# Finer waits between scalings and additions, and two other places in VectorE's order, in an attention trunk

## The chip, the cores and the metric

The kernel runs on one core of one Trainium2 chip. The metric is the device time of one execution in microseconds (us); the median of several runs counts. TensorE does the matrix products (PE in the profile, its loads of stationary operands PEld), VectorE (DVE) and ScalarE (ACT) the elementwise work, SyncE (SP) issues most loads and stores, GpSimd (POOL) some others.

## The reference

```python
D_MODEL, SEQ, DEPTH, N_MIXERS, N_HEADS = 4096, 256, 1, 2, 32     # HEAD_DIM = 128

def attn_branch(xn, w_in, w_out):
    q, k, v, g = split(xn @ w_in, 4)                # w_in: 4096 x 16384
    o = stick_breaking_attention(q, k, v)           # per head; log-space, suffix sums over the keys
    return (o * silu(g)) @ w_out                    # w_out: 4096 x 4096

def reference(x, norm_attn, w_in_attn, w_out_attn, ..., final_norm):
    h = x
    for i in range(DEPTH):                          # DEPTH is 1: only i = 0, the attention layer
        if i % N_MIXERS == 0:
            h = h + attn_branch(rms_norm(h, norm_attn), w_in_attn, w_out_attn)
        ...
    return rms_norm(h, final_norm)
```

All is float32, for 256 rows (two tiles of 128). The convolution layer's inputs are not used at this depth.

## The kernel before, in words

**Products.** A float32 product is made of three fp32r matmuls (`mm3`): each operand is split into a high part (a cast on ScalarE: `wh<-raw`) and a low part (a subtraction on VectorE: `wl<-raw,wh`), and high x high, high x low and low x high are added in PSUM. Each weight tile that is loaded (`raw`) thus costs a cast and a subtraction before TensorE can use it.

**Units and steps.** The work is cut into 20 units, each a strip of output columns with four blocks: two tiles of rows by two blocks of 512 columns. Units 0 to 15 are the input projection (two heads' q, k, v and gate each), units 16 to 19 the output projection (1024 of the 4096 output columns each). A unit runs over the inner dimension in 16 steps. Units 0 and 16 are plain, with eight products a step. The others are "mixed": a step is either of eight products or of seven, a Strassen-like scheme in which sums of weight blocks (additions on VectorE, `raw<-raw,raw`, and accumulating loads on POOL) save one product. Such a unit gathers its products in seven PSUM banks, b1 to b7, and the four output blocks are combinations of the banks.

**Combining.** At a unit's end `combine` makes the four blocks. `two[0]` starts as a copy of bank 1 and gets bank 6 added; `two[1]` is `two[0]` plus bank 7; `one[0]` is a scaled copy of bank 1, `one[1]` a scaled copy of `two[1]`. In the attention units the scale is the row's RMS factor; there `two[1]` and `two[0]` are then scaled in place on ScalarE (`scaled`). Last, banks 2 and 4 are added to `one[0]` and `one[1]`, bank 5 to `two[1]` and `two[0]`, bank 3 to `two[0]` (`add_scaled`, a scale-and-add on VectorE in the attention units, a plain addition in the others). `nc.give("b4")` and the like free a bank for the next unit. A mixed unit's first step and its last are of eight products, into banks 2, 2, 4, 4, 5, 5, 3, 3. In the attention units `one` is `qk_sb` and `two` is `gv_sb` in the profile; in the output units both are `h`.

**Who sets the order.** The whole program is written by a planner (`Plan`). Each piece of work is a Python generator that waits for names (`nc.until`), takes and gives places in rings of buffers (`nc.take`, `nc.give`), tells names (`nc.tell`) and asks for an engine with a cost and a key. A planned engine that comes free takes, of the requests that are ready, the one with the smallest key (a planned time); an idle engine takes any. The instructions are emitted in that order, and on the chip each engine runs its own in that order, waiting only for the semaphores of its operands and buffers. A wait in the plan is therefore not a wait on the chip, but it decides which instruction stands ahead of which.

**The output units.** `blocks_out` runs in units 17 to 19, for the two columns' blocks that the unit before has made. For each column block it loads the gain of the last norm once (`grow`), and for each of the two row tiles in turn: loads the residual rows (`xres`), adds them (`h<-h,xres`), sums the squares on ScalarE (`sq<-h`), and multiplies by the gain (`h<-h,grow`, `gain_on`). The addition's key is the place of a step of the unit, `H_LATER` steps behind steps 0, 2, 4 and 6; the multiplication's is `GAIN_LATER` us behind that. `grow` and `xres` live in the ring "gh" with four places. When all is done `blocks_out` tells `("h", c)`; in the last unit `last_h` waits for that, then loads the last two gains and forms the last columns, and `finish` scales the rows by the RMS factor and stores them.

Of the kernel before, what the change touches and what calls it, by code (L numbers as in the profile page):

```python
# [61 lines left out]
SPREAD = (10, 1.0)  # L62
HEADS_AHEAD = 0
SUMS_LATER = 2
H_LATER = 6
GAIN_LATER = 8.0
ON_SCALAR = ((1, 3, 5), (1, 3))
AHEAD, SUMS_AHEAD = 6.0, 3.0
BLOCKS_LATER = 2
# [179 lines left out]
def kernel(  # L249
# [10 lines left out]
    nc = Plan(tc)  # L260
# [22 lines left out]
    OUT0 = len(units)  # L283
# [38 lines left out]
    def place_at(u, s):  # L322

        return place_of[u + int(s // NS), step_at(u + int(s // NS), int(s % NS))]
# [5 lines left out]
    def dve(emit, n, key=None, more=0, **kw):  # L330
        n = n if isinstance(n, tuple) else (n,)
        cost = sum(vector_ns(m) for m in n) + 122 * (len(n) - 1) + more
        return nc.work("vector", cost, emit, soon() if key is None else key, **kw)

    def act(emit, n, key=None, **kw):
        n = n if isinstance(n, tuple) else (n,)
        cost = sum(scalar_ns(m) for m in n) + 100 * (len(n) - 1)
        return nc.work("scalar", cost, emit, soon() if key is None else key, **kw)
# [21 lines left out]
    def together(*works):  # L360
        for w in works:
            nc.start(w)
# [346 lines left out]
    def combine(u, one, two, what):  # L709

        bank = ev[u]
        key = place_of[u + 1, 0] - SOONER * 1e3

        row = [rs["v"][:, t : t + 1] if u < OUT0 else 1.0 for t in range(NT)]

        def add(to, b, f, n):
            return dve(lambda: nc.vector.tensor_tensor(out=to, in0=bank[b], in1=f, op=ALU.add), W, key + n)

        def add_scaled(to, b, f, n, t):
            if u >= OUT0:  # L720
                return add(to, b, f, n)
            return dve(
                lambda: nc.vector.scalar_tensor_tensor(
                    out=to, in0=bank[b], scalar=row[t], in1=f, op0=ALU.mult, op1=ALU.add
                ),
                W, key + n, more=60,
            )

        def scaled(to, f, t):
            return act(lambda: nc.scalar.activation(to, f, AF.Copy, scale=row[t]), W, key - 2e3)  # L730

        yield act(lambda: nc.scalar.copy(two[:, 0, :], bank[1]), W, key - 2e3)
        yield scaled(one[:, 0, :], bank[1], 0)
        nc.give("b1")

        def early():
            yield nc.until(("full", u, 6))
            yield add(two[:, 0, :], 6, two[:, 0, :], 0)
            nc.give("b6")
            yield nc.until(("full", u, 7))  # L740
            yield add(two[:, 1, :], 7, two[:, 0, :], 0)
            nc.give("b7")
            yield scaled(one[:, 1, :], two[:, 1, :], 1)
            if u < OUT0:
                for t in (1, 0):
                    yield scaled(two[:, t, :], two[:, t, :], t)
            nc.tell(("early", u))

        def first_():
            yield nc.until(("full", u, 2))  # L750
            yield add_scaled(one[:, 0, :], 2, one[:, 0, :], 1, 0)
            nc.give("b2")
            yield nc.until(("full", u, 4), ("early", u))
            yield add_scaled(one[:, 1, :], 4, one[:, 1, :], 2, 1)
            nc.give("b4")
            nc.tell((what[0], u))

        def second():
            yield nc.until(("full", u, 5), ("early", u))
            for t in (1, 0):  # L760
                yield add_scaled(two[:, t, :], 5, two[:, t, :], 3, t)
            nc.give("b5")
            yield nc.until(("full", u, 3))
            yield add_scaled(two[:, 0, :], 3, two[:, 0, :], 4, 0)
            nc.give("b3")
            nc.tell((what[1], u))

        together(early(), first_(), second())

    def out_of(u):  # L770
# [257 lines left out]
    def load_gain(c):  # L1028
        grow[c] = wp.tile([P, W], F32, tag="gh", name=f"grow{c}", bufs=ROWS)
        return moved(  # L1030
            "sync", lambda: nc.sync.dma_start(grow[c], gain_out[:, c * W : (c + 1) * W].partition_broadcast(P)), [W],
            soon(), after=lambda: nc.tell(("grow", c)),
        )
# [13 lines left out]
    def gain_on(c, t, key=None):  # L1047
        h = hs[c, t]
        yield nc.until(("grow", c))
        yield dve(lambda: nc.vector.tensor_tensor(out=h, in0=h, in1=grow[c], op=ALU.mult), W, key)  # L1050

    def block_out(c, t, key):

        h = hs[c, t]
        yield nc.take("gh")
        yield load_out(c, t)
        yield nc.until(("xres", c, t))
        yield nc.take("att")
        yield dve(lambda: nc.vector.tensor_tensor(out=h, in0=h, in1=xres[c, t], op=ALU.add), W, key)
        nc.give("gh")  # L1060
        yield from squares(c, t, c, ALL, key)
        nc.give("att")
        yield from gain_on(c, t, key + GAIN_LATER * 1e3)

    def blocks_out(u, c):

        for d in range(2):
            for t in range(NT):
                yield nc.until(("used", u, step_at(u, 2 * (NT * d + t))), ("C", u - 1))
                if t == 0:  # L1070
                    yield nc.take("gh")
                    yield load_gain(c + d)
                key = place_at(u, 2 * (NT * d + t) + H_LATER)
                yield from block_out(c + d, t, key)
# [260 lines left out]
```

## Time and profile before

| | us |
|---|---|
| time, median of 3 runs | 1699.11 (1698.87 to 1699.47) |
| the profiled execution's own time | 1699.48 |
| its span, first to last instruction | 1697.7 |
| TensorE (PE) busy | 1681.1, 99% |
| weight loads (PEld) busy | 1417.1, 83% |
| VectorE (DVE) busy | 1602.2, 94% |
| ScalarE (ACT) busy | 1206.3, 71% |

The mean granted TensorE clock was 0.998. A row of a group gives busy time, mean time of one, and the idle time of the engine ahead of it with what ended it. A row of waits reads: who waited, for whom, us in total, times, longest. A row of the windows gives, after the window and its length, each engine's busy time with its count of instructions, the granted clock, and DMA's share and rate. A row of the timeline gives start, duration, engine, operation and, in brackets, the idle time before it and what ended it. Matmuls overlap, and their ends are modelled: the starts tell more than the busy times.

### The profile page before, as it was taken

The page shows a single profiled execution, that of the slowest core. Times are in us where ns is not written, and L with a number is a line of the kernel's source. Part 1 is how long each engine was busy: PE and PEld are TensorE (multiplying, and loading weights), DVE is VectorE, ACT ScalarE, POOL GpSimd, SP SyncE. Part 2 cuts the span into 40 slices and gives each one's busy share as a digit, 9 for nine tenths or more (in the row PEclk, how much of TensorE's full clock was granted, in tenths as well). Part 3 has the DMA queues.
Part 4 walks back from the last instruction along what each step waited for, and adds up shares of the span by engine and source line. Part 5 has one row for each costly group of instructions (what it writes and reads, how often), then busy time and mean ns, then how long its engine had stood idle before and what let it go on. Part 6 is the DMA issues. An engine that isn't in the chain of part 4 may idle for free. (4 is left out here: it accounts for less than half of the span.)

```text
span 1697.7 us, 25128 instructions
## 1 busy us (share of the span) xinstructions
PE 1681.1 (99%) x7776; PEld 1417.1 (83%) x7776; DVE 1602.2 (94%) x2025; ACT 1206.3 (71%) x1665; POOL 324.9 (19%) x400
## 2 busy tenths in 40 slices
PE   9999999999999999999999999999999999999997
PEld 7888888888888888888888888888888888888885
DVE  8889999999999999999999999999999978999997
ACT  8986767777767676767676767676867765656654
POOL 0022222122212222221222121212121111212110
PEclk9999999999999999999999999999999999999999
DMA  9979788878787879797979797979797978788895
GB/s 340 332 198 248 228 245 228 249 218 252 217 251 218 263 200 267 201 272 198 272 203 267 196 271 201 267 200 266 214 253 201 307 231 265 245 246 258 245 299 191
DMA packets 248438, 412.77 MB, mean 243 GB/s; under 512 B 28016, under 2 KB 72560, under 8 KB 248304
## 3 DMA queue, kind: packets, MB, share of 16 engines
q1 hardware_dynamic: 194544, 354.24, 62.5%
q0 software_dynamic: 53472, 56.65, 20.3%
q8 instruction: 61, 1.00, 0.2%
q14 instruction: 73, 0.60, 0.1%
q10 hardware_dynamic: 288, 0.28, 0.1%
HBM read 402.93 MB, written 8.13 MB: 242 GB/s over the span
## 5 line engine op out<-in xcount | busy, mean ns | idle before, releaser
L132 ACT CAST wh<-raw 128x1024 fp32r<-128x1024 f32 (+1 forms) x989 | 919.3, 970 | 383.8 <-DVE raw L132 166.3
L132 DVE TENSOR_TENSOR wl<-raw,wh 128x1024 fp32r<-128x1024 f32 (+1 forms) x815 | 974.3, 1217 | 50.7 <-ACT wh L132 22.7
L132 PE MATMUL acc<-wh,sh 128*128 128x512 f32 x2048 | 771.8, 389 | 1.3 <-ACT wh L132 1.3
L132 PE MATMUL acc<-wh,sl 128*128 128x512 f32 x1898 | 726.8, 383 | 0.0
L132 PE MATMUL acc<-wl,sh 128*128 128x512 f32 x1748 | 669.0, 383 | 0.0
L132 PEld LDWEIGHTS acc<-wh,sh 128*128 128x128 f32 x2048 | 383.9, 188 | 79.5 <-PE acc L132 4.7
L132 POOL DMA_DIRECT2D raw<-in_w_in_dram x300 | 258.4, 953 | 974.4 <-DMA raw<-in_w_in_dram 390.6
L132 PEld LDWEIGHTS acc<-wh,sl 128*128 128x128 f32 x1898 | 355.9, 188 | 64.4 <-DVE sl L132 0.2
L132 PEld LDWEIGHTS acc<-wl,sh 128*128 128x128 f32 x1748 | 328.4, 188 | 56.0 <-DVE wl L132 0.4
L132 DVE TENSOR_TENSOR raw<-raw,raw 128x512 f32<-128x512 f32 x348 | 236.9, 684 | 13.1 <-DMA raw<-in_w_in_dram 10.7
L132 PE MATMUL acc<-wh,oh 128*128 128x512 f32 x512 | 192.2, 383 | 0.3 <-DVE gv_sb L132 0.3
L132 PE MATMUL acc<-wh,ol 128*128 128x512 f32 x488 | 186.4, 382 | 0.0
L132 PE MATMUL acc<-wl,oh 128*128 128x512 f32 x464 | 177.4, 382 | 1.2 <-DVE wl L132 1.2
L132 DVE TENSOR_TENSOR wh<-raw,wh 128x512 fp32r<-128x512 f32 x174 | 118.9, 683 | 3.3 <-ACT wh L132 2.6
L132 DVE TENSOR_TENSOR raw<-raw 128x512 f32<-128x512 f32 x174 | 118.7, 682 | 0.0
L132 PEld LDWEIGHTS acc<-wh,oh 128*128 128x128 f32 x512 | 96.0, 187 | 17.8 <-DVE gv_sb L132 0.7
L132 PEld LDWEIGHTS acc<-wh,ol 128*128 128x128 f32 x488 | 91.4, 187 | 16.0
L132 PEld LDWEIGHTS acc<-wl,oh 128*128 128x128 f32 x464 | 87.0, 187 | 17.5 <-DVE wl L132 2.1
L132 POOL DMA_DIRECT2D raw<-in_w_out_dram x48 | 41.5, 977 | 174.0 <-DMA raw<-in_w_out_dram 62.2
L132 ACT ACTIVATE f<-f 128x384 f32<-128x384 f32 x96 | 50.5, 526 | 3.0
L132 POOL DMA_DIRECT2D p<-spill x27 | 16.5, 655 | 88.4 <-DVE ol L132 21.0
L132 DVE SCALAR_TENSOR_TENSOR gv_sb<-acc,scalars,gv_sb 128x512 f32<-128x512 f32 x45 | 33.4, 742 | 0.0
(86 smaller groups left out, 764.3 us busy)
## 6 DMA issues: line engine op xcount, KB each, us to landing
raw<-in_w_in_dram SPq DMA_DIRECT2D x1024, 256.0 KB, 4.5
raw<-in_w_out_dram SPq DMA_DIRECT2D x256, 256.0 KB, 4.5
raw<-in_w_in_dram POOLq DMA_DIRECT2D x300, 128.0 KB, 5.2
p<-spill POOLq DMA_DIRECT2D x27, 256.0 KB, 5.1
raw<-in_w_out_dram POOLq DMA_DIRECT2D x48, 128.0 KB, 5.3
xr<-in_x_dram SPq DMA_DIRECT2D x16, 256.0 KB, 5.4
xres<-in_x_dram SPq DMA_DIRECT2D x16, 256.0 KB, 5.7
out_dram<-h SPq DMA_DIRECT2D x16, 256.0 KB, 2.9
```

What stands on the lines that cost most here:

```text
L132: return self.tc.keep_in_program_order(getattr(self.engine, name)(*args, **kw))
```

## The change

Three edits. In `combine`, `early` tells its first name as soon as `one[1]` has been scaled, and a name for each of `two[1]` and `two[0]` once that one has been scaled; the addition of bank 4 waits for the first of these, and each addition of bank 5 for the name of the block that it adds to. In the output units, where nothing is scaled, these names are told at the same moment as before. `H_LATER` goes from 6 to 3 steps, `GAIN_LATER` from 8 to 30 us; both act in units 17 to 19.

```diff
-H_LATER = 6
-GAIN_LATER = 8.0
+H_LATER = 3
+GAIN_LATER = 30.0
...
             yield scaled(one[:, 1, :], two[:, 1, :], 1)
-            if u < OUT0:
-                for t in (1, 0):
+            nc.tell(("early", u))
+            for t in (1, 0):
+                if u < OUT0:
                     yield scaled(two[:, t, :], two[:, t, :], t)
-            nc.tell(("early", u))
+                nc.tell(("early", u, t))
...
         def second():
-            yield nc.until(("full", u, 5), ("early", u))
+            yield nc.until(("full", u, 5))
             for t in (1, 0):
+                yield nc.until(("early", u, t))
                 yield add_scaled(two[:, t, :], 5, two[:, t, :], 3, t)
             nc.give("b5")
```

## The prediction

> **What bounds the kernel.** I read the page's busy table first, then the waits of PE (matmuls) and of PEld (its weight loads), then the busy time in 40 us windows.
>
> ```profile
> span 1697.7 us, 25128 instructions
> ...
> PE 1681.1 (99%) x7776; PEld 1417.1 (83%) x7776; DVE 1602.2 (94%) x2025; ACT 1206.3 (71%) x1665; POOL 324.9 (19%) x400
> ...
> L132 PE MATMUL acc<-wh,sl 128*128 128x512 f32 x1898 | 726.8, 383 | 0.0
> ```
>
> ```profile
> PE acc L132 <- ACT wh L132: 1.3, 1, 1.3
> PE acc L132 <- DVE wl L132: 1.2, 2, 1.0
> PE acc L132 <- DVE gv_sb L132: 0.3, 1, 0.3
> ...
> PEld acc L132 <- PE acc L132: 4.7, 14, 0.4
> PEld acc L132 <- DVE qk_sb L132: 4.7, 14, 0.3
> ```
>
> ```profile
> 1320.00:1360.00 40.00, 39.72 (x184) 33.41 (x184) 39.97 (x49) 30.78 (x39) 6.75 (x10) 1.00 0.97 308
> ...
> 1480.00:1520.00 40.00, 39.72 (x180) 33.46 (x180) 38.86 (x45) 25.74 (x32) 7.77 (x9) 1.00 0.87 251
> ...
> 1560.00:1600.00 40.00, 39.04 (x177) 32.81 (x176) 39.24 (x48) 26.37 (x34) 7.99 (x10) 1.00 0.85 252
> ```
>
> TensorE is the bound: after the first 40 us it stands visibly in only these three windows, 0.28, 0.28 and 0.96 us, at the full granted clock (1.00). The order of work can thus win only what TensorE loses by waiting, and the tail. But a matmul counts as busy for 383 ns while the next one starts 220 ns after it, so a late start under about 160 ns shows no idle time at all. The PEld waits give these away: two kinds, 14 times each, 0.3 us a time. Fourteen is the number of borders between the attention units 1 to 15. The timeline of PE at one border (unit 9 to 10) shows what they cost:
>
> ```profile
> 850.78 0.38 PE L132 MATMUL acc<-wl,sh 128*128 128x512 f32 x1
> 851.00 0.39 PE L132 MATMUL acc<-wh,sl 128*128 128x512 f32 x1
> 851.31 0.48 PE L132 MATMUL acc<-wh,sh 128*128 128x512 f32 x1
> 851.64 0.38 PE L132 MATMUL acc<-wl,sh 128*128 128x512 f32 x1
> ...
> 852.98 0.38 PE L132 MATMUL acc<-wh,sl 128*128 128x512 f32 x1
> 853.32 0.46 PE L132 MATMUL acc<-wh,sh 128*128 128x512 f32 x1
> 853.62 0.38 PE L132 MATMUL acc<-wl,sh 128*128 128x512 f32 x1
> 853.84 0.39 PE L132 MATMUL acc<-wh,sl 128*128 128x512 f32 x1
> ```
>
> The normal step is 0.22 us (850.78 to 851.00). At 851.31 two steps in a row are 0.31 and 0.33: 0.20 us lost. At 853.32 they are 0.34 and 0.30: another 0.20 us. A unit begins with products into banks 2, 2, 4, 4, 5, 5, 3, 3, three matmuls each; the matmul at 851.00 is the sixth, so the unit began at 851.00 - 5 x 0.22 = 849.9, the first stall is the first product into bank 4, the second the first into bank 5. Both wait for the old unit's sums in these banks to be read out. Bank 5 is my reading: the view names PE there, which had long been done.
>
> **The new waits in `combine`.** The same border on VectorE, then on ScalarE:
>
> ```profile
> 846.20 0.68 DVE L132 TENSOR_TENSOR gv_sb<-acc,gv_sb 128x512 f32<-128x512 f32 x1
> ...
> 849.37 1.23 DVE L132 TENSOR_TENSOR wl<-raw,wh 128x1024 fp32r<-128x1024 f32 x1
> 850.51 0.75 DVE L132 SCALAR_TENSOR_TENSOR qk_sb<-acc,scalars,qk_sb 128x512 f32<-128x512 f32 x1
> 851.17 0.74 DVE L132 SCALAR_TENSOR_TENSOR gv_sb<-acc,scalars,gv_sb 128x512 f32<-128x512 f32 x1
> ...
> 852.43 0.74 DVE L132 SCALAR_TENSOR_TENSOR gv_sb<-acc,scalars,gv_sb 128x512 f32<-128x512 f32 x1
> ...
> 854.22 0.74 DVE L132 SCALAR_TENSOR_TENSOR gv_sb<-acc,scalars,gv_sb 128x512 f32<-128x512 f32 x1
> ```
>
> ```profile
> 846.92 0.72 ACT L132 ACTIVATE qk_sb<-gv_sb,scalars 128x512 f32<-128x512 f32 x1 [1.54 <-DVE gv_sb L132]
> 847.67 0.72 ACT L132 ACTIVATE gv_sb<-gv_sb,scalars 128x512 f32<-128x512 f32 x1
> ...
> 849.24 0.72 ACT L132 ACTIVATE gv_sb<-gv_sb,scalars 128x512 f32<-128x512 f32 x1
> ```
>
> Bank 4's addition (850.51) reads only the scaling that ended at 847.64 (846.92 + 0.72). It was placed after the last scaling (849.24 + 0.72 = 849.96), and a `wl` of 1.2 us had been taken at 849.37. PE resumed at 851.31, right behind it. The planner can now release it at about 847.8 (scaling seen; bank 4 was full at about 847.4: four products, 12 x 0.22 = 2.6 us, lie between it and 849.9). With VectorE free every 0.6 to 1.2 us, it starts by 849 and ends by 849.7, some 1.5 us before PE asks at about 851.2. Stall gone: 14 x 0.20 = 2.8 us. Bank 5 needs two additions: the first can follow from 848.8, the second only after the scaling that ends at 849.96. With one foreign instruction slipped in (at most 1.2 us) the second ends between 850.8 and 852; PE asks at about 852.9. Stall gone: another 2.8 us. Bank 3's addition (854.22) then moves forward too, to end by 854. The same at the border from unit 15 to 16: the window 1320 to 1360 has 0.28 us idle; adding the hidden 0.16 and a late second step (0.33 instead of 0.22, as at 851.64) makes 0.55; I take 0.5.
>
> No instruction is added or removed (VectorE stays at 2025, ScalarE at 1665). Displaced are the `wl` at 849.37 and its neighbours, by at most four additions, 4 x 0.66 = 2.6 us; a `wl` feeds products some microseconds ahead, and PE waited for one only twice in the whole run (1.2 us), in the out-projection. I cost this at nothing; without that cover it would be up to 2.6 us a border. The attention heads of the old unit also start some 2 us sooner: the same instructions, elsewhere.
>
> **H_LATER 6 to 3, GAIN_LATER 8 to 30.** These touch units 17 to 19. The residual addition `h<-h,xres` becomes urgent three steps (about 15 us) sooner, the multiplication by the final gain `h<-h,grow` 30 - 8 - 15 = 7 us later. A key only ranks what is ready: a free VectorE takes the multiplication anyway.
>
> ```profile
> 1578.15 0.68 DVE L132 TENSOR_TENSOR h<-h,grow 128x512 f32<-128x512 f32 x1
> ...
> 1670.26 0.69 DVE L132 TENSOR_TENSOR h<-h,grow 128x512 f32<-128x512 f32 x1
> ...
> 1673.07 1.23 DVE L132 TENSOR_TENSOR wl<-raw,wh 128x1024 fp32r<-128x1024 f32 x1 [0.99 <-ACT wh L132]
> 1674.21 1.41 DVE L132 TENSOR_TENSOR h<-acc,h 128x512 f32<-128x512 f32 x2
> 1676.31 2.50 DVE L132 TENSOR_TENSOR h<-h,xres 128x512 f32<-128x512 f32 x4 [0.69 <-ACT h L132]
> ```
>
> ```profile
> 1579.43 2.28 DVE wl L132 x2
> 1581.72 0.04 issue
> 1581.76 90.20 PE acc L132 x407
> ```
>
> The chain of waits runs through VectorE until 1581.72, then through PE: that is the 0.96 us idle, with the hidden part 1.2 us. A gain multiplication at 1578.15 stands right ahead of the `wl` that released PE; putting it later takes 0.6 us off, putting it and one neighbour later takes all. The stall in the window 1480 to 1520 (0.28, with the hidden part 0.55) may go or stay likewise. Bounds: a gain of 1.75 us and, since the sooner additions can stand before a tight `wl`, a loss of about the same. I take a gain of 0.9, nearer to the gain, because no late unit can have more than its eight such instructions ahead of the tight place and at least one is put off.
>
> In the last unit the block at 1674.21 (the last columns' sums) is planned only after the last gain (1670.26). That gain may come 1.7 us later at no cost: VectorE waits 0.99 and 0.69 us there. Each microsecond beyond moves the end. I take nothing. SP's queue is affected: a load of `xres` or of the gain waits for its buffer, and weight loads stand behind it.
>
> ```profile
> SPq L132 <- DVE h L132: 9.4, 7, 3.1
> ```
>
> Seven such waits, 3.1 us at most; seven raw buffers cover them, else it is up to 3.1 us each. POOL's reloads of `p` share these buffers and are likewise covered unless a gain is held very long.
>
> **Sum.** 2.8 + 2.8 + 0.5 + 0.9 = 7.0 us. The profiled execution took 1699.48 us (span 1697.7), 0.37 above the median of 1699.11; so 1692.5 there and 1692.1 by the median.
>
> **A rule against it.** VectorE is busy 94%, PEld 83% (first fence). The Trainium skill, "Perfetto Trace Analysis", Identifying the Most-Contended Engine, judges VectorE by its busy share but TensorE by its weight loads; by that rule VectorE is the bound, and an edit that only reorders its work brings nothing: 1699.1 instead of 1692.1. The trace speaks against it: VectorE is idle for 95 us while PE's matmuls step at 0.22 us nearly throughout; only the window 1560 to 1600 agrees.
>
> **The rivals.**
> 1. VectorE binds, so PE's stalls only move: what is won at a border is lost at the next late `wl`. For it: 39.97 of 40 us busy in 1320 to 1360. Against: its idle time elsewhere. 1699.1.
> 2. Only bank 4's stall goes; the second addition from bank 5 stays late, since its scaling still ends at 849.96 and foreign work slips in. Sum without 2.8: 1694.9.
> 3. The last unit's gain waits until its key is due, 7 us later; 1.7 are covered, 5.3 reach the output stores: 1699.1 - 7.0 + 5.3 = 1697.4.
> 4. Slower: the heads' first scores come sooner, and TensorE waits in order for ScalarE's copy of `qkT`, which stands behind a cast that waits for VectorE's sums.
>
> ```profile
> 852.60 1.05 ACT L132 CAST wh<-raw 128x1024 fp32r<-128x1024 f32 x1 [1.70 <-DVE raw L132]
> 853.55 0.58 ACT L132 COPY qkT<-tr 128x512 f32<-128x512 f32 x1
> ...
> 854.73 0.82 PE L132 MATMUL z<-qkT 128*128 128x128 f32 x4
> ```
>
> The margin is 854.73 - 854.13 = 0.6 us. If the copy keeps its place behind such a cast while the tiles to be turned are ready 2 us sooner, PE stands up to 1.7 - 0.6 = 1.1 us at each of 15 units: 16.5 us, giving 1708.6. It decides the sign from (7.0 + 3.4) / 15 = 0.7 us a unit. Against it: PE waits for no `qkT` today, and copy and scores are moved together.
>
> **Chances and range.** Forecast 0.68, rival 1 0.10, rival 2 0.10, rival 3 0.06, rival 4 0.06. About 3.4 us (0.2%) is what a measurement can tell from no change. Forecast and rival 2 are faster: 0.78; rivals 1 and 3 within it: 0.16; rival 4 slower: 0.06. The lowest time is all stalls gone: 5.6 + 0.55 + 1.75 = 7.9, so 1691.2; with 0.3 for the tail 1690.9. The top takes in rivals 2 and 3: 1697.5. The forecast's own range is 1690.9 to 1694.
>
> **What would show it.** The waits of PEld lose both rows of 14 (or one: rival 2); the steps 0.31/0.33 and 0.34/0.30 at each border become 0.22; the scale-and-add into `qk_sb` stands before the last scaling of `gv_sb`; windows 1480 to 1520 and 1560 to 1600 show PE nearer 40. The prediction is wrong if waits of PE on `z`, `tr` or `wl` appear in units 2 to 15, or if the time from the last matmul to the end grows.

## The result and the profile after

The changed kernel takes 1693.98 us (median of 8 runs, 1693.27 to 1695.18), the kernel before 1698.97 us beside it (8 runs, 1698.18 to 1699.63): a ratio of 0.9969, 95% interval 0.9960 to 0.9979, or 5.0 us. The prediction was 1692.1 us, so the gain is 2 us smaller than forecast; the median lies at the upper end of the forecast's own range, 1690.9 to 1694. The profiled execution of after took 1693.27 us, the lowest of its eight.

Span, busy table and chain on the page of after:

```profile
span 1691.6 us, 25185 instructions
...
PE 1674.7 (99%) x7776; PEld 1418.6 (84%) x7776; DVE 1600.5 (95%) x2025; ACT 1202.2 (71%) x1665; POOL 325.3 (19%) x400
...
PE 96%; DVE 2%; DMA 1%; issue 1%; ACT 0%; SPq 0%; DVEq 0%; ACTq 0%
```

The counts of the engines are those of before. 96% of the chain that ended last is now TensorE. What PEld waits for (who, for whom, us in total, times, longest):

```profile
PEld L132 <- DVE idle L132: 3.6, 10, 1.3
PEld acc L132 <- DVE sl L132: 2.3, 2, 2.1
PEld acc L132 <- DVE wl L132: 1.7, 3, 1.2
PEld acc L132 <- ACT wh L132: 0.8, 1, 0.8
```

Both rows of 14 are gone, the one on `qk_sb` and the one put down to PE. The border from unit 9 to 10 shows why. In after, unit 10 begins at 846.77. VectorE there, then ScalarE, then PE:

```profile
844.60 0.74 DVE L132 SCALAR_TENSOR_TENSOR qk_sb<-acc,scalars,qk_sb 128x512 f32<-128x512 f32 x1
845.35 0.75 DVE L132 SCALAR_TENSOR_TENSOR gv_sb<-acc,scalars,gv_sb 128x512 f32<-128x512 f32 x1
846.02 1.21 DVE L132 TENSOR_TENSOR wl<-raw,wh 128x1024 fp32r<-128x1024 f32 x1
847.15 0.74 DVE L132 SCALAR_TENSOR_TENSOR gv_sb<-acc,scalars,gv_sb 128x512 f32<-128x512 f32 x1
```

```profile
843.47 0.72 ACT L132 ACTIVATE qk_sb<-gv_sb,scalars 128x512 f32<-128x512 f32 x1 [0.98 <-DVE gv_sb L132]
...
845.79 0.72 ACT L132 ACTIVATE gv_sb<-gv_sb,scalars 128x512 f32<-128x512 f32 x1
```

```profile
849.90 0.39 PE L132 MATMUL acc<-wl,sh 128*128 128x512 f32 x1
850.13 0.38 PE L132 MATMUL acc<-wh,sl 128*128 128x512 f32 x1
850.35 0.40 PE L132 MATMUL acc<-wh,sh 128*128 128x512 f32 x1
850.58 0.39 PE L132 MATMUL acc<-wl,sh 128*128 128x512 f32 x1
```

Bank 4's addition (844.60) runs before the last scaling (845.79) and 2.2 us before the unit begins; before the change it started 0.6 us after the begin. The first product into bank 5 starts at 850.35 with the normal step. The second addition from bank 5 ended at 847.89, 2.5 us ahead of it.

Where the time went, section by section. The times are my count from the starts of the matmuls in each trace; the tail runs from the start of the last matmul to the end of the span.

| us | to unit 1 | units 1 to 16 | unit 17 | unit 18 | unit 19 | tail | span |
|---|---|---|---|---|---|---|---|
| before | 94.22 | 1350.80 | 79.21 | 80.01 | 80.56 | 12.91 | 1697.7 |
| after | 93.66 | 1345.36 | 78.63 | 79.93 | 80.46 | 13.52 | 1691.6 |
| new waits, old keys | 93.76 | 1345.06 | 78.63 | 79.75 | 81.00 | 12.73 | 1690.9 |
| new keys, old waits | 93.34 | 1351.01 | 78.63 | 80.67 | 80.72 | 16.47 | 1700.8 |
| bank 4's wait alone | 93.37 | 1344.31 | 79.19 | 80.30 | 80.59 | 12.62 | 1690.4 |
| bank 5's wait alone | 93.53 | 1359.66 | 79.19 | 80.39 | 80.67 | 12.61 | 1706.1 |
| after, root first | 93.05 | 1345.44 | 78.63 | 79.83 | 80.46 | 12.63 | 1690.0 |

The attention units give 5.44 us. Units 17 to 19 and the tail together give 252.69 - 252.54 = 0.15 us: unit 17 wins 0.58, the tail loses 0.61. The period of a unit, from its begin to the next one's, falls from 84.02 to 84.08 us (units 2 to 15) to 83.71 us (units 3 to 14).

### The profile page after: what moved, and what is told of

The parts are those of the page before. It is cut to its first block, busy times and chain, and to the rows that moved or that the text cites. A ratio compares the mean times of both kernels' runs of the same rounds, so it can differ in the third digit from the quotient of the medians.

```text
span 1691.6 us, 25185 instructions
## 1 busy us (share of the span) xinstructions
PE 1674.7 (99%) x7776; PEld 1418.6 (84%) x7776; DVE 1600.5 (95%) x2025; ACT 1202.2 (71%) x1665; POOL 325.3 (19%) x400
## 4 chain that ended last, share of the span: by engine, by line
PE 96%; DVE 2%; DMA 1%; issue 1%; ACT 0%; SPq 0%; DVEq 0%; ACTq 0%
PE acc L132 91%; PE z L132 3%; PE o L132 1%; PE tr L132 1%; DVE wl L132 1%; DVE h L132 1%; DVE raw L132 0%; DMA raw<-in_w_in_dram 0%; DMA xres<-in_x_dram 0%; ACT wh L132 0%; DMA raw<-in_w_out_dram 0%; SPq L132 0%; DVE scalars L132 0%; ACT sq L132 0%; DVE wh L132 0%
```

## The experiments

Theory A: the gain is the new waits in `combine`; the two keys give next to nothing. Rivals: the keys carry part of it; only one of the two banks matters; the gain comes from the heads' transposition of q and k ("the turn", `tr` in the profile), which moves from 2.2 us after a unit's begin to 0.36 us before it.

**New waits, old keys.** After with

```diff
-H_LATER = 3
-GAIN_LATER = 30.0
+H_LATER = 6
+GAIN_LATER = 8.0
```

> The new waits in combine alone; H_LATER 6 and GAIN_LATER 8 as before. Theory A (the two bank waits carry the gain): both rows of 14 PEld waits are gone, units 1 to 16 are 5.4 us shorter as in the changed kernel, the time is 1693.3 to 1694.0, the same as the changed kernel within 0.5 us; the stall near 1516 stays and the tail from the last matmul to the end is back at 12.9 us. Rival B (the two keys carry a part of it): 1695 to 1697.

1693.24 us (1692.53 to 1698.22), ratio 0.9973 (0.9963 to 0.9984). The whole gain is there without the keys. Unit 17 takes 78.63 us here too: the stall in the window 1480 to 1520, which the prediction had given to the keys and which I had expected to stay here, is gone. The new keys with the old waits remove it as well (78.63), and with only one of the two waits or one of the two keys it stays (79.19 to 79.35), so it can't be put down to either edit.

**New keys, old waits.** Before with `H_LATER = 3`, `GAIN_LATER = 30.0`.

> H_LATER 3 and GAIN_LATER 30 alone, the old waits in combine. Theory A: both rows of 14 PEld waits stay; unit 17 is 0.6 us shorter, unit 18 at most 0.1, and the tail 0.6 us longer if the keys cause it, so 1698.5 to 1699.2, no difference. Rival B: 1696 to 1697.5.

1702.29 us (1701.45 to 1704.87), ratio 1.0020 (1.0011 to 1.0029): slower by 3 us, which neither of my two expectations had. Both rows of 14 stay (4.8 and 4.7 us). The table puts the loss in unit 18 (+0.66) and the tail (+3.56). Its chain of waits, then POOL's timeline, then VectorE's near the end:

```profile
1564.49 6.15 DMA xres<-in_x_dram
1581.30 103.48 PE acc L132 x467
```

```profile
1624.57 0.57 POOL L132 DMA_DIRECT2D p<-spill  x1 [3.51 <-DMA xres<-in_x_dram]
```

```profile
1680.83 1.62 DVE L132 TENSOR_TENSOR h<-acc,h 128x512 f32<-128x512 f32 x3 [0.91 <-PE acc L132]
...
1684.81 0.76 DVE L132 TENSOR_TENSOR h<-acc,h 128x256 f32<-128x256 f32 x2 [1.57 <-PE acc L132]
...
1686.38 1.68 DVE L132 TENSOR_SCALAR h<-h,scalars 128x512 f32<-128x512 f32 x4
```

A load of the residual is on the chain in unit 18: the addition that was to come sooner waits for it. In unit 19 the last reload of `p` waits 3.51 us for a residual's transfer; the two share the ring of four buffers. At the end VectorE waits twice for TensorE with additions of the last columns, 0.91 us at 1680.83 and 1.57 us at 1684.81. The factor of the first rows, whose root ScalarE had ready at 1683.59, stands behind the second pair, so these rows are scaled at 1686.38, 3.6 us later than before (1682.76), where the factor stood ahead of that pair.

**Each key alone.** Before with `H_LATER = 3`, and before with `GAIN_LATER = 30.0`.

> The kernel before with H_LATER 3 alone (old waits, GAIN_LATER 8). Together the two keys cost 3.3 us, nearly all of it between the start of the last unit's final matmuls and the end. Theory G: the loss comes from the later gain, because the buffer of the gain is handed on only after its second multiplication, so the next residual load starts late. Then this run is like the kernel before, 1699 us (1698 to 1700), with the time from the last matmul's start to the end near 12.9 us. Theory H: the residual additions that come sooner push the reloads of p and the sums of the last unit back. Then this run is near 1702.3 us with some 16 us behind the last matmul.

> The kernel before with GAIN_LATER 30 alone (old waits, H_LATER 6). Theory G (late gain holds its buffer): near 1702.3 us, the time behind the last matmul near 16 us instead of 12.9. Theory H (sooner residual additions): 1699 us. If both this run and the one with H_LATER 3 are near 1699 us, the loss needs both keys, and it is an accident of the order that they make together.

1698.82 us (ratio 0.9998, 0.9989 to 1.0007) and 1697.52 us (0.9990, 0.9981 to 0.9999), tails 12.63 and 12.61 us. Neither theory G nor theory H holds: each key alone costs nothing, and the loss needs both. That is the third outcome of the expectation. The chain and the rows above show by which order the two lose; why the planner falls into it only with both was not followed further.

**Bank 4's wait alone.** Against after, with the old keys: bank 5 waits, as before the change, until both blocks have been scaled.

```diff
             yield nc.until(("full", u, 5))
+            yield nc.until(("early", u, 0))
             for t in (1, 0):
-                yield nc.until(("early", u, t))
```

> Keys as before; only the addition of bank 4 waits for its own scaling, the additions of bank 5 wait for both scalings. Theory A with the second stall at bank 5: the waits on qk_sb are gone, the other row of 14 stays, half of the gain, 1696.0 to 1696.6. Rival C (the second stall belongs to the heads' turning of tiles, which starts as soon as bank 4 is added, and not to bank 5): both rows go, 1693.3 to 1694.0.

1693.05 us (1692.30 to 1696.11), ratio 0.9966 (0.9954 to 0.9978). I had expected half the gain; it is all there. What PEld waits for, then VectorE at the same border (unit 10 begins at 845.98), then PE:

```profile
PEld L132 <- DVE idle L132: 3.6, 10, 1.3
PEld acc L132 <- DVE wl L132: 3.0, 4, 1.6
PEld acc L132 <- DVE sl L132: 1.9, 2, 1.7
```

```profile
843.79 0.75 DVE L132 SCALAR_TENSOR_TENSOR qk_sb<-acc,scalars,qk_sb 128x512 f32<-128x512 f32 x1
...
846.25 0.75 DVE L132 SCALAR_TENSOR_TENSOR gv_sb<-acc,scalars,gv_sb 128x512 f32<-128x512 f32 x1
...
847.51 0.75 DVE L132 SCALAR_TENSOR_TENSOR gv_sb<-acc,scalars,gv_sb 128x512 f32<-128x512 f32 x1
```

```profile
849.31 0.38 PE L132 MATMUL acc<-wh,sl 128*128 128x512 f32 x1
849.52 0.38 PE L132 MATMUL acc<-wh,sh 128*128 128x512 f32 x1
849.75 0.39 PE L132 MATMUL acc<-wl,sh 128*128 128x512 f32 x1
```

Bank 5's additions still wait for the last scaling, yet the second ends at 848.26, 1.3 us before the first product into that bank (849.52). Before the change they ran at 851.17 and 852.43, behind bank 4's at 850.51. So bank 5 was late because three additions stood in a row on VectorE behind one scaling; with bank 4's taken out of the row, the other two are in time. Against the unit's begin they run 1.0 us sooner: 0.66 us is the place that bank 4's addition no longer takes (850.51 to 851.17 before), the rest goes with the last scaling, which ends 0.29 us ahead of the begin instead of 0.07 us behind it.

**Bank 5's wait alone.** Against after, with the old keys: bank 4 waits, as before the change, until all has been scaled; each addition of bank 5 waits for its own scaling.

```diff
-            yield nc.until(("full", u, 4), ("early", u))
+            yield nc.until(("full", u, 4), ("early", u, 0))
```

> Keys as before; only the additions of bank 5 wait each for its own scaling, the addition of bank 4 waits for both. Theory A: the waits on qk_sb stay (14 times), the other row goes, 1696.0 to 1696.6. Rival C: the heads start as late as before, so the second stall stays and nothing is won, 1698.5 to 1699.2.

1704.18 us (1703.97 to 1709.25), ratio 1.0040 (1.0027 to 1.0052): slower by 5 us. PEld's waits, PE's waits, then VectorE some 16 us ahead of the border and at it, then PE (unit 10 begins at 853.49):

```profile
PEld acc L132 <- issue: 13.0, 14, 2.0
```

```profile
PE acc L132 <- DVE qk_sb L132: 6.7, 8, 1.7
```

```profile
837.34 0.69 DVE L132 TENSOR_TENSOR raw<-raw,raw 128x512 f32<-128x512 f32 x1 [1.48 <-DMA raw<-in_w_in_dram]
...
853.03 0.75 DVE L132 SCALAR_TENSOR_TENSOR gv_sb<-acc,scalars,gv_sb 128x512 f32<-128x512 f32 x1
853.75 1.23 DVE L132 TENSOR_TENSOR wl<-raw,wh 128x1024 fp32r<-128x1024 f32 x1
854.89 0.75 DVE L132 SCALAR_TENSOR_TENSOR qk_sb<-acc,scalars,qk_sb 128x512 f32<-128x512 f32 x1
```

```profile
854.60 0.39 PE L132 MATMUL acc<-wh,sl 128*128 128x512 f32 x1
855.78 0.47 PE L132 MATMUL acc<-wh,sh 128*128 128x512 f32 x1 [0.80 <-DVE qk_sb L132]
...
856.55 0.60 PE L132 MATMUL tr<-ident,qk_sb 128*128 128x128 f32 x4
...
857.45 0.38 PE L132 MATMUL acc<-wh,sl 128*128 128x512 f32 x1
857.66 0.40 PE L132 MATMUL acc<-wh,sh 128*128 128x512 f32 x1
```

Bank 5's first addition (853.03) and the `wl` behind it stand in front of bank 4's (854.89), and TensorE, which asks for bank 4 first, starts it 1.18 us after the matmul before instead of 0.22 (0.31 before the change). In the profiled execution that order alone costs no more than the old one: at eight of the fourteen borders the step into bank 4 is 0.54 us, and with the late step behind it (0.30) 0.40 us are lost, as much as at both banks together before the change. At the other six, the one shown among them, the step is 0.80 to 2.05 us, and each of these six stands behind a wait of VectorE of 1.09 to 2.51 us, some 16 us earlier, at a sum of weights: five times for a late transfer (837.34 above), once for something that the profile does not name. Ahead of the eight this wait is 0.67 us at most. The profiled execution took 1707.76 us, 3.6 more than the median, so its rows show where time is lost and not how the median's 5 us divide.

The turn stands where it stood before the change, between the first products into banks 4 and 5 (856.55), and the first product into bank 5 (857.66) starts with the normal step. The rival that the turn made it thus fails.

**The tail.** The changed kernel, with one wait added where the last block's banks are read out:

```diff
         yield nc.until(("full", LAST, b), *(["C12"] if b == 3 else ()))
+        if b == 2:
+            yield nc.until(("most", NT - 1))
```

> The changed kernel; in the last block bank 2's addition is planned only after the sum of squares of the other tile of rows has been joined. Theory: the 0.6 us that the changed kernel spends more behind its last matmul (13.5 against 12.9 us) come from that addition and its squares standing ahead of the root of the other tile. Then the tail is 12.9 us or less and the time 0.6 us below the changed kernel's 1694.0. Rival: the tail is set by the length of the stores and of the last factor; then it stays at 13.5 and the time at 1694.0.

> The changed kernel with bank 2's addition of the last block behind the joined sum of the other rows, once more, since the profiled execution of its first run lost 3.9 us in units 3 and 4 and 2.7 us before unit 1. Theory: those losses are of that one execution's transfers and do not come back, units 3 and 4 take 83.7 us, the tail is 12.6 us, the time 0.6 to 0.9 us below the changed kernel on this chip. Rival: the order itself makes the losses (it is the same up to the last block), then they are here again.

1693.17 us (1691.62 to 1699.30, ratio 0.9962, 0.9948 to 0.9976), and on another chip 1692.59 us (1691.76 to 1697.53, 0.9967, 0.9955 to 0.9980); the table of sections shows the second run. The tail is 12.63 us both times. ScalarE in after, then in this kernel (second run):

```profile
1675.29 0.60 ACT L132 ACTIVATE sq<-h 128x512 f32<-128x512 f32 x1 [0.73 <-DVE scalars L132]
...
1675.92 0.28 ACT L132 ACTIVATE scalars<-squares_of_rows,scalars 128x1 f32<-128x1 f32 x1
```

```profile
1673.96 0.29 ACT L132 ACTIVATE scalars<-squares_of_rows,scalars 128x1 f32<-128x1 f32 x1
...
1674.60 0.60 ACT L132 ACTIVATE sq<-h 128x512 f32<-128x512 f32 x1
```

In after the squares of the last columns (1675.29) stand ahead of the root (1675.92) that the finished row tile waits for; here the root is first. That is the 0.9 us. In its first run the profiled execution was the slowest, 1699.30 us; its loss is told at the end.

**The gain left out in unit 18.** The changed kernel without the four multiplications by the final gain in unit 18; the columns that unit 17 made go out without the gain.

```diff
-        yield from gain_on(c, t, key + GAIN_LATER * 1e3)
+        if c not in (2, 3):
+            yield from gain_on(c, t, key + GAIN_LATER * 1e3)
```

> The changed kernel without the four multiplications by the final gain in unit 18 (the columns that unit 17 made are left without the gain; its loads stay). Theory V: the 1.2 us late start near 1575 us is a shortage of VectorE's time, 39.97 of 40 us busy there. Four multiplications are 2.7 us: the late start goes, and unit 18 takes 1.0 to 1.2 us less (78.8 instead of 79.9), the time is 1692.9 us. Theory O: it is a place in the order (one sum or a tight wl ahead of which something stands); then the stall stays within 0.3 us or moves, and the time is 1694.0 us.

1692.13 us (1691.80 to 1694.45), ratio 0.9961 (0.9948 to 0.9974). PE in after, VectorE in after, then PE here:

```profile
1575.01 0.49 PE L132 MATMUL acc<-wl,oh 128*128 128x512 f32 x1 [0.77 <-DVE wl L132]
```

```profile
1571.40 0.68 DVE L132 TENSOR_TENSOR h<-h,xres 128x512 f32<-128x512 f32 x1
1572.00 0.68 DVE L132 TENSOR_TENSOR raw<-raw 128x512 f32<-128x512 f32 x1
1572.60 5.76 DVE L132 TENSOR_TENSOR wl<-raw,wh 128x1024 fp32r<-128x1024 f32 x5
```

```profile
1573.93 0.49 PE L132 MATMUL acc<-wl,oh 128*128 128x512 f32 x1
```

The step ahead of that matmul falls from 1.17 to 0.45 us and unit 18 from 79.93 to 79.17. But unit 19 takes 80.99 instead of 80.46: some late starts come back there. The two units together win 0.23 us; the rest of the 1.5 us between the spans is the tail, which takes 12.62 us here, and the start. Theory V holds for the place, not for the sum: 2.7 us less work for VectorE gave TensorE 0.23 us.

**After and three variants on one chip.** The four run once more beside each other.

> The changed kernel once more, beside its variants on the same chip. By the sections of its first trace (units 1 to 16, 17, 18, 19, tail: 1345.4 + 78.6 + 79.9 + 80.5 + 13.5 = 1597.9 us) it should be the slowest of the four of this call, by 0.5 to 1 us.

> Finer waits, old keys, on the same chip as the changed kernel: 1597.15 us by the sections of its first trace, thus 0.7 us below the changed kernel. If the keys are worth the 0.9 us of the prediction, it is 0.9 us above it.

> Old keys, finer wait for bank 4 alone, on the same chip as the changed kernel: 1597.0 us by the sections of its first trace, thus 0.9 us below the changed kernel and level with the kernel that has both waits. If bank 5's own finer wait is worth anything, it is slower than that one.

| | us | ratio to before |
|---|---|---|
| after | 1693.90 (1692.82 to 1694.36) | 0.9967 (0.9955 to 0.9980) |
| after, root first | 1692.59 (1691.76 to 1697.53) | 0.9967 (0.9955 to 0.9980) |
| new waits, old keys | 1694.15 (1692.76 to 1696.00) | 0.9972 (0.9961 to 0.9984) |
| bank 4's wait alone, old keys | 1692.92 (1692.34 to 1695.23) | 0.9965 (0.9951 to 0.9978) |

All four are about 5 to 6 us faster than before. Bank 4's wait alone and root first have medians about 1 us below the changed kernel's, but the intervals overlap, so neither is shown to beat the changed kernel. The order expected of new waits with old keys did not come: unit 3 of its profiled execution took 84.82 us instead of 83.71.

## Why the prediction was right, and where it was off

**TensorE is the bound, and late starts too short to show as idle time cost it 0.4 us a border.** Right. Gone are both rows of 14, and units 1 to 16 win 5.44 us.

**Banks 4 and 5, 2.8 us each, and 0.5 at the border from 15 to 16.** The sum of 6.1 measured 5.44 in after and 6.49 with bank 4's wait alone. In after a unit (3 to 14) wins 0.31 to 0.37 us instead of 0.40. Of its matmuls some start 0.23 to 0.24 us after the one before instead of 0.22 (850.13 behind 849.90), and I could not settle why.

**Bank 5's own wait.** The bank was named rightly: before the change the load of weights for its first product started 0.11 to 0.12 us behind the end of its second addition at each of the fourteen borders. Its cause was half wrong: the prediction gave the second 2.8 us to the split of bank 5's wait. The split of bank 4's wait alone brings all of it, since bank 4's addition stood in front. The split of bank 5's wait alone frees bank 5 and makes bank 4 later by as much, and the kernel is 5 us slower, in the profiled execution where VectorE waits for late transfers ahead of the border. The prediction added two terms that were not independent; its sum came out because one edit removes both stalls. Rival 2, which kept bank 5 late because its scaling ends late, fails on the same runs.

**The keys, 0.9 us, and the tail, nothing.** This is the term that failed. Units 17 to 19 and the tail measured 0.15 us together. Unit 17's 0.58 us comes without the keys too, and with the keys without the waits. In unit 18 the multiplication was indeed put later, but `H_LATER` put a residual addition of the same 0.68 us in its place (1571.40 above, ahead of the five `wl` that TensorE waits for): a swap. The prediction looked at what moved away from the tight place and not at what moved in. And the tail grew by 0.61 us, one of the signs named beforehand for the prediction being wrong; the run with the root first shows the squares ahead of the root as its cause. With the old waits the keys cost 3 us.

**The sum.** The profiled execution went from 1699.48 to 1693.27 us, against 1692.5 forecast: 0.66 less at the borders and 0.75 less from the keys and tail, while 0.56 came from ahead of unit 1, where the program is the same. The median of after lies another 0.7 us above its profiled execution.

**The rivals.** Rival 1 (VectorE binds) took up the rule of the Trainium skill, "Perfetto Trace Analysis", Identifying the Most-Contended Engine. VectorE was 94% busy before and is 95% busy after, and 5 us came from its order alone, so for the attention units the rule fails here. For one stretch it holds. The windows of after, then of the kernel without the gain in unit 18 (window and length, then busy time of PE, PEld, DVE, ACT and POOL):

```profile
1480.00:1520.00 40.00, 40.00 (x183) 34.03 (x182) 39.23 (x49) 23.76 (x29) 6.93 (x8) 1.00 0.88 259
...
1560.00:1600.00 40.00, 39.23 (x177) 32.80 (x176) 39.97 (x50) 25.96 (x34) 8.09 (x10) 1.00 0.92 263
```

```profile
1560.00:1600.00 40.00, 39.90 (x179) 33.16 (x179) 38.46 (x48) 24.54 (x33) 8.05 (x10) 1.00 0.89 262
```

In 1480 to 1520 PE is full. In 1560 to 1600 VectorE is busy 39.97 of 40 us and PE still stands 0.77; take VectorE's work away and PE gets 0.67 of it back. Rival 3 did not come with the new waits. With the old waits both keys lengthened the tail by 3.56 us, but by another path: the last gain came 3.5 us later (1673.79 against 1670.26) and moved the last columns' sums by 0.18 us only (1674.39 against 1674.21), and the loss was the factor behind additions that wait for TensorE. Rival 4 did not come: PE waits for no `z` in the attention units, and the turn and the scores both moved ahead. A wait on `tr`, another of the signs named beforehand, did come once, 0.6 us at the end of unit 7 in the second profile of after; the last section tells of it.

The Trainium skill, "Perfetto Trace Analysis", Optimization Strategy, says that a gap which repeats on the saturated engine can mean too little SBUF or PSUM for the next tile. That fits the look of this one (28 stalls of 0.2 us, each at a bank not yet free). The runs show another cause: no bank was added, and the order of the read-outs on VectorE removed the stalls.

## What to carry to other kernels

When a dependency is made finer, put the new order in the order in which the next consumer asks: giving the bank that TensorE needs first its own wait brought all of the gain, while giving only the second bank its own wait moved the stall from one bank to the other, and the kernel was 5 us slower. A shared wait hides which addition is the late one, and two stalls behind it are not two terms of a sum. When a key moves work away from a tight place, look up what moves into that place, and which rings of buffers the moved work holds meanwhile.

## What the runs showed that I had not expected

With the finer waits a late transfer can reach TensorE. In the first run of "after, root first", one sum of weights on VectorE waited 3.35 us for its transfer, and some 16 us later the turns of that border waited. VectorE, then PE:

```profile
332.42 0.69 DVE L132 TENSOR_TENSOR raw<-raw,raw 128x512 f32<-128x512 f32 x1 [3.35 <-DMA raw<-in_w_in_dram]
```

```profile
348.07 0.33 PE L132 MATMUL tr<-ident,qk_sb 128*128 128x128 f32 x1 [0.89 <-DVE qk_sb L132]
...
349.33 0.66 PE L132 MATMUL tr<-ident,qk_sb 128*128 128x128 f32 x3 [0.93 <-DVE qk_sb L132]
```

Units 3 and 4 took 86.17 and 85.16 us in that execution and 83.71 in the second run of the same kernel, so the order alone does not make the loss. Single units of 84.5 to 84.8 us appear also in after (unit 7, second profile, behind a wait of 2.20 us) and with the old keys (unit 3, second profile, behind one of 3.06). Such transfers were late before too. VectorE's waits in the kernel before:

```profile
DVE raw L132 <- DMA raw<-in_w_in_dram: 10.7, 10, 1.7
```

Yet there no period of units 2 to 15 was off by more than 0.06 us from another. One difference is where the wait stands. With the old waits it comes, but for one of 0.59 us, 36 to 39 us into a unit, some 46 us ahead of the next border, and in the run with the new keys and the old waits even one of 2.45 us (unit 6) left the periods of units 2 to 15 at 84.09 to 84.11 us. With both finer waits it comes, but for two of 0.31 and 0.49 us, 66 to 69 us into the unit, 15 to 18 us ahead of the border: waits of up to 1.54 us lengthen a period by less than 0.1 us, and those of 1.75 to 3.35 us lengthen the unit and the next one together by 0.16 to 3.9 us. With bank 5's wait alone it comes there too (67 to 69 us) and gets through at bank 4, although the turn stands 2.4 us or more behind the unit's begin (2.2 before the change), so the earlier turn is not needed for it. With bank 4's wait alone no such wait is longer than 0.81 us in either profile. Why the wait moved within the unit was not followed, and no experiment changed its place alone.
